# Moving a second conv pair of a hybrid decoder layer into the seven-product stage, with new orders at the start and around it

## The chip, the cores and the metric

The kernel runs on one core of a Trainium2 chip. The core has a matrix engine (TensorE, PE in the profile), a vector engine (VectorE, DVE), an activation engine (ScalarE, ACT), a general-purpose engine (GpSimd, POOL) and a queueing engine (SyncE, SP); 16 DMA engines carry transfers between its memory and the chip's. The metric is the time of one execution in microseconds on the device.

## The reference

One decoder layer of 1024 positions with a model width of 1024, all in float32 (cut to what matters):

```python
h = rms_norm(x, g_mix)
z = einsum("bsd,de->bse", h, w_in) + b_in          # 1024 -> 7168 columns
va, ga, xb, gb, sa, sb = split(z)                  # 1024, 1024, 1536, 1536, 1024, 1024
u = causal_depthwise_conv(va * sigmoid(ga), conv_a_w, conv_a_b)     # width 31
y_a = silu(layer_norm(u, ln_g, ln_b)) @ w_a_out
v = causal_depthwise_conv(xb, conv_b_w, conv_b_b)                   # width 4
v = rg_lru(v, ...)         # 16 heads of 96 channels, gates, h_t = a_t * h_(t-1) + b_t
y_b = (v * gelu(gb)) @ w_b_out
m = sigmoid(sa) * y_a + sigmoid(sb) * y_b
x = x + m @ w_o
f = square(relu(rms_norm(x, g_mlp) @ w_1))         # 1024 -> 4096
out = rms_norm(x + f @ w_2, g_final)
```

## The kernel before

**Matmuls.** Every matrix factor is split into a high and a low part, and a product is three matmuls: high by high, high by low, low by high. Weights are the stationary side (128x128), activations the moving side (128x512). Positions lie along the free axis.

**Tables.** `GA + j`, `VA + j`, `XB + t`, `GB + t`, `SA + j`, `SB + j` are numbers of column blocks of 128 of `z`. The in-projection has two parts. In the first, each block is one *slot* of plain matmuls (`chunk_mm`, L725, 48 of them into two banks). The table `CH` lists the blocks in order, `NC1` is their number, and slots `s` run from 3 on, as the first three blocks are made by `first_z` (L258) at the kernel's start. In the second part, blocks go in pairs listed in `ZPAIRS`, and each pair is made by a seven-product scheme (`z_mm`, L929): seven steps of 12 matmuls in place of two times 48. The scheme needs sums of weights (`zs`, on DVE), their split halves (`zo`), and sums of the activations (`xs`) split into `xs4` to `xs7`, in two halves each.

**Splitting.** `split_dma` copies the negated source into the low tile on ACT (L65), lets a POOL-issued DMA add the source to it (L66), and copies the high part on ACT (L67). For other tiles DVE subtracts the high part (L462 is a helper that issues queued vector work). So a `zo` tile is ready when the POOL-issued transfer has landed.

**Recurrent part.** Slots also hold the heads of the recurrent layer: gates on ACT (L542), and per group of three 128-channel tiles an exponential round (L558, L559), a root round (L566) and scans on DVE (`scan_tile`: L575, L576, L577, L578). `HS0` gives each head its slot, `EXP` the slots of the exponential rounds. A scanned tile goes to memory (`hd`) and comes back as `hb` to be multiplied with gelu of a `GB` block (L969, L972).

**Conv part.** `u_out` makes `u = (va + b) * sigmoid(ga + b)` (sigmoid on ACT at L587), and DVE does the width-31 convolution between other work (L637). The second part's `VA` pair does the same in `z_u` (L944).

**Order.** All of it is written out by hand and by a planner in the source: `clk` holds planned clocks of the engines, `later` queues vector work with a planned ready time and a planned cost, and `XS`, `ZX`, `ZL` are tables of steps at given slots. On the chip an engine executes its instructions in this order and waits on semaphores.

**Later stages.** After the second part come `yb` (L1129), `y_a` and the output projection (L1427), the up projection (`gu` products and `f` products, L1427 and L1709), and the down projection (L2002). `up_load` (L1664) loads a block of `w_1` as `raws[i, kk]`; `GX` is a table of its extra steps.

Of the kernel before, what the change touches and what calls it, by code (L numbers as in the profile page):

```python
# [30 lines left out]
def trunk_kernel(ctx: ExitStack, tc: tile.TileContext, x, xt_in, xt_eo, vecs, w_in, w_a_out, w_b_pl, w_b_sq,  # L31
# [97 lines left out]
    gmix = cp.tile([P, 16], F32, name="gmix")  # L129
    nc.sync.dma_start(gmix[:, 0:8], vecs[:, 0:8])  # L130
    nc.gpsimd.dma_start(vec, vecs)
# [31 lines left out]

    load_w0(0)
    for c2 in range(4):
        load_xc(0, c2)
# [18 lines left out]

    def x_square(t, eng):
# [5 lines left out]
        if eng is nc.vector:  # L192
            nc.vector.scalar_tensor_tensor(a, a, 1.0, a, ALU.mult, ALU.mult, accum_out=ss)
        else:
            nc.scalar.activation(a, a, AF.Square, accum_out=ss)
# [47 lines left out]
    def first_w(i, part):  # L243
        if part == "h":
            if i < 2:
                wh = wp.tile([P, 8, P], F32R, tag="wh", name=f"w{i}_h")
                wl = wp.tile([P, 8, P], F32R, tag="wl", name=f"w{i}_l")
            else:
                wh, wl = (T(f"w{i}_{n}", F32R).rearrange("p (k c) -> p k c", c=P) for n in "hl")
            w0.append((wh, wl))  # L250
            z0.append(PS(f"z{16 + i}"))
            nc.scalar.activation(wh, raw0[i], AF.Copy)
        else:
            nc.vector.tensor_tensor(w0[i][1], raw0[i], w0[i][0].bitcast(F32), ALU.subtract)

    def first_z(i, hf, k, which):
# [78 lines left out]
    with tc.manual_schedule(engines={mybir.EngineType.Activation, mybir.EngineType.DVE,  # L335
# [4 lines left out]

        spare = PS("spare", "ps2")

# [37 lines left out]
        for c in range(9):  # L380
# [5 lines left out]
            if 3 <= c < 7:  # L386
                x_square(c - 3, nc.scalar)
            if c:
# [195 lines left out]

    def u_gate(j, ps):
        ut[j] = u = T(f"u{j}")
        nc.scalar.activation(u.rearrange("p (o n) -> p o n", o=2), ps.rearrange("p (n o) -> p o n", o=2),  # L587
                             AF.Sigmoid, bias=bin_c[:, GA + j:GA + j + 1])
        return at("A", 1.11)

    def u_mul(j, ps, ready=0):
        uv = ut[j].rearrange("p (o n) -> p o n", o=2)
        later(ready, 1.28, nc.vector.scalar_tensor_tensor, uv, ps.rearrange("p (n o) -> p o n", o=2),
              bin_c[:, VA + j:VA + j + 1], uv, ALU.add, ALU.mult)
        fresh.append(j)

    def u_out(j, psv, psg):
        u_mul(j, psv, u_gate(j, psg))

# [191 lines left out]
    def z_get(n, f):  # L791
# [17 lines left out]
    with tc.manual_schedule(engines=ENGINES):  # L809
        for s in range(3, NC1):  # L810
# [33 lines left out]
            elif c >= GA:  # L844
                if CH[s] == c - GA + VA:
                    u_gate(c - GA, zps[s - 1])
                else:
                    u_out(c - GA, zps[s - 2], zps[s - 1])
            w_parts(s + 1)
# [170 lines left out]

    ZX = {0: ((x_parts, 1, 7),), 2: ((x_parts, 1, 5),), 4: ((x_parts, 1, 4),)}
    H_AT = {2: (0, 0), 5: (1, 1), 3: (0, 1), 4: (1, 0)}
    with tc.manual_schedule(engines=ENGINES):
# [155 lines left out]
        z_get(3, z_lhs)  # L1179
        u_mul(NU - 1, zps[NC1 - 1])  # L1180
        vector_work(clk["V"])
# [588 lines left out]
    def g_get(n, f):  # L1770
# [511 lines left out]
```

## Time and profile before

| What | Value |
|---|---|
| median of 3 runs | 1531.3 us (1531.1 to 1531.85) |
| profiled execution, own time | 1531.15 us |
| its span | 1529.4 us, clock 0.999 |
| PE busy | 1519.5 us, 6722 matmuls |
| DVE busy | 1200.0 us |
| ACT busy | 928.3 us |
| POOL busy | 192.3 us |

The span is the time between the first and the last instruction that the profile shows; the execution's own time is 1.75 us longer. By matmul lines, the stages lie so on the time axis: start and first three blocks to 43 us; plain slots 43 to 339; second part of the in-projection 339 to 627; `yb` 627 to 757; `y_a` and output projection 757 to 907; up 907 to 1217; down 1217 to 1522. *Z* below is the moment when the second part begins on PE, 339.29 us.

A row of the timeline has start, duration, engine, line, operation, output<-input, the tile's shape, a count where several equal ones are merged, and in brackets the engine's idle time before it with what ended it.

### The profile page before, as it was taken

Reading aid. Unit: us, or ns where it says so; the run is one execution under the profiler, and the core shown is the slowest. Engines: PE = TensorE matmul, PEld = TensorE weight load, DVE = VectorE, ACT = ScalarE, POOL = GpSimd, SP = SyncE. Lnnn points to the kernel's source line nnn. Section 1 sums busy time; section 2 is a strip of 40 time slices with the busy share of each in tenths; the row PEclk is TensorE's granted clock in tenths of the full one; section 3 lists DMA queues with packets and bytes.
Section 4 is the critical chain, followed back from the end, with each engine's and each line's share of the span. In section 5 each row is a group of like instructions: output and inputs, shape, how many; then the busy total and the mean of one; then the engine's idle time right before and its main releaser. Section 6 shows DMA issues by size and latency. Waiting matters only on the chain.

```text
span 1529.4 us, 18963 instructions
## 1 busy us (share of the span) xinstructions
PE 1519.5 (99%) x6722; PEld 1251.2 (82%) x6722; DVE 1200.0 (78%) x1636; ACT 928.3 (61%) x1299; POOL 192.3 (13%) x228
## 2 busy tenths in 40 slices
PE   9999999999999999999999999999999999999998
PEld 7878887888888888888888887888888888888886
DVE  6899996998999997788869879755555387777777
ACT  6748688576566667645575777554444455545475
POOL 0111011022222222000022332000000000101010
PEclk9999999999999999999999999999999999999999
DMA  9766779797997889964879897333333974776465
GB/s 352 188 146 154 184 159 204 196 258 209 265 261 173 186 207 271 297 226 119 269 201 302 188 205 195 138 122 111 111 111 111 302 265 131 177 211 169 107 123 153
DMA packets 130799, 296.53 MB, mean 194 GB/s; under 512 B 12896, under 2 KB 34912, under 8 KB 130704
## 3 DMA queue, kind: packets, MB, share of 16 engines
q1 hardware_dynamic: 98960, 215.92, 42.0%
q0 software_dynamic: 31600, 79.15, 28.1%
q8 instruction: 52, 0.85, 0.2%
q14 instruction: 43, 0.35, 0.1%
q10 hardware_dynamic: 144, 0.26, 0.0%
HBM read 149.79 MB, written 60.82 MB: 138 GB/s over the span
## 4 chain that ended last, share of the span: by engine, by line
PE 96%; issue 2%; DVE 1%; POOL 1%; DMA 0%; ACT 0%; POOLq 0%; ACTq 0%
PE z L725 16%; PE z L258 2%; PE d1b L2002 2%; PE d2b L2002 2%; PE d0b L2002 2%; PE d3b L2002 2%; PE d0e L2002 1%; PE d3e L2002 1%; PE d3a L2002 1%; PE d2e L2002 1%; PE d2a L2002 1%; PE d1e L2002 1%; PE d1a L2002 1%; PE d0a L2002 1%; PE rg L532 1%
## 5 line engine op out<-in xcount | busy, mean ns | idle before, releaser
L725 PE MATMUL z<-xh,win_h 128*128 128x512 f32 x368 | 115.4, 391 | 0.0
L725 PE MATMUL z<-xl,win_h 128*128 128x512 f32 x368 | 114.9, 390 | 0.0
L637 DVE SCALAR_TENSOR_TENSOR y<-u,vec,y 128x511 f32<-128x511 f32 (+14 forms) x120 | 88.2, 735 | 0.0
L725 PE MATMUL z<-xh,win_l 128*128 128x512 f32 x368 | 87.4, 389 | 0.0
L637 DVE SCALAR_TENSOR_TENSOR yt<-u,vec,yt 128x511 f32<-128x511 f32 (+6 forms) x112 | 82.5, 736 | 0.0
L637 DVE SCALAR_TENSOR_TENSOR y<-yt,csum,y 128x511 f32<-128x511 f32 (+6 forms) x112 | 82.4, 736 | 0.0
L725 PEld LDWEIGHTS z<-xh,win_h 128*128 128x128 f32 x368 | 69.1, 188 | 16.0 <-ACT win_h L67 0.5
L725 PEld LDWEIGHTS z<-xl,win_h 128*128 128x128 f32 x368 | 69.1, 188 | 14.9
L725 PEld LDWEIGHTS z<-xh,win_l 128*128 128x128 f32 x368 | 69.1, 188 | 14.6
L542 ACT ACTIVATE g<-rg,vec 96x1024 f32<-96x1024 f32 x32 | 35.5, 1110 | 72.9 <-PE rg L534 72.8
L1697 ACT ACTIVATE o<-s 128x512 fp32r<-128x512 f32 x56 | 33.7, 623 | 45.7 <-DVE s L1681 26.4
L66 POOL DMA_DIRECT2D zo<-zw x45 | 39.2, 871 | 133.8 <-ACT zo L65 110.4
L483 DVE SCALAR_TENSOR_TENSOR v<-xb,vec,v 128x1023 f32<-128x1023 f32 (+2 forms) x36 | 46.2, 1282 | 6.3 <-ACT v L474 5.3
L66 POOL DMA_DIRECT2D db_10l<-br x4 | 3.5, 877 | 339.6 <-DMA br<-in_w_dram 254.4
L66 POOL DMA_DIRECT2D win_l<-win_raw x23 | 20.0, 868 | 194.0 <-ACT win_l L65 155.9
L65 ACT ACTIVATE zo<-zw 128x512 fp32r<-128x512 f32 x45 | 28.2, 626 | 24.3 <-PE z10f L929 2.1
L1219 DVE TENSOR_TENSOR o<-s,o 128x512 fp32r<-128x512 f32 x56 | 37.2, 683 | 1.3 <-ACT o L1697 1.3
L66 POOL DMA_DIRECT2D zo<-zs x30 | 26.4, 879 | 75.9 <-ACT zo L65 63.8
L67 ACT ACTIVATE zo<-zw 128x512 fp32r<-128x512 f32 x45 | 27.9, 621 | 0.0
L578 DVE TENSOR_TENSOR_SCAN g<-a,g 128x1024 f32<-128x1024 f32 x12 | 27.5, 2291 | 0.4
L66 POOL DMA_DIRECT2D ga<-gsa x8 | 7.0, 874 | 161.0 <-DMA m<-mbd 150.8
L1219 DVE TENSOR_TENSOR o<-w_raw,o 128x512 fp32r<-128x512 f32 x38 | 25.9, 683 | 0.0
(3182 smaller groups left out, 4912.0 us busy)
## 6 DMA issues: line engine op xcount, KB each, us to landing
w_raw<-in_w_dram SPq DMA_DIRECT2D x34, 512.0 KB, 5.7
br<-in_w_dram SPq DMA_DIRECT2D x32, 512.0 KB, 6.1
ar<-fd SPq DMA_DIRECT2D x32, 512.0 KB, 7.0
zw<-in_w_in_dram SPq DMA_DIRECT2D x28, 512.0 KB, 6.9
win_raw<-in_w_in_dram SPq DMA_DIRECT2D x23, 512.0 KB, 5.0
win_l<-win_raw POOLq DMA_DIRECT2D x23, 512.0 KB, 5.2
zo<-zw POOLq DMA_DIRECT2D x45, 256.0 KB, 5.7
gates<-zg SPq DMA_DIRECT2D x32, 256.0 KB, 4.1
```

The source lines that it names most:

```text
L65: nc.scalar.activation(l, src, AF.Copy, scale=-1.0)
L66: nc.gpsimd.dma_start(l, src, accum_op=ALU.add)
L67: nc.scalar.activation(h, src, AF.Copy)
L258: nc.tensor.matmul(z0[i][:, HALVES[hf]], w0[i][w][:, k, :], xpart(a, hf, k), start=k == 0 and which == "hh", stop=k == 7 and which == ("hl ...
L483: nc.vector.scalar_tensor_tensor(v[:, d:S], a[:, 0:S - d], cbw_c[:, w * 12 + t:w * 12 + t + 1], v[:, d:S], ALU.mult, ALU.add)
L542: nc.scalar.activation(a, gps.pop((n, gi))[:HD, :], AF.Sigmoid, bias=(ba_c, bx_c)[gi][:, n:n + 1])
L578: nc.vector.tensor_tensor_scan(i, a, i, 0.0, ALU.mult, ALU.add)
L637: nc.vector.scalar_tensor_tensor(o[:, k:], a[:, 0:HS - k], c, o[:, k:], ALU.mult, add)
L725: nc.tensor.matmul(zps[s][:, HALVES[hf]], w[:, k, :], xw[k][part][hf], start=n == 0, stop=n == 23)
L1219: tt(l, src, h.bitcast(F32), ALU.subtract)
L1697: nc.scalar.activation(o[:, 0], src, AF.Copy)
L2002: nc.tensor.matmul(o, a, b, start=start and n == 0, stop=stop and n == len(todo) - 1, skip_group_check=not start or not stop)
```

## The change

1. The pair `GA + 6`, `VA + 6` leaves the plain slots (`NU` 7 to 6, `NC1` 26 to 24) and becomes a pair of the second part (15 pairs to 16). The second part's order mixes gate (`SA`), conv (`VA`) and recurrent (`GB`) pairs where before all `GB` pairs came first.
2. The plain slots are put in another order. The heads lose one of their two gaps, and the last exponential rounds start at slots 17 and 21 instead of 18 and 22.
3. Parts of the activation sums (`x_parts`) and the scan of tile 11 go from the slots into the second part.
4. At the start the first weight block and the first activation block are loaded in halves from two queues, the first split is made in halves, one of four squares goes from ACT to DVE, 14 small decay operations go behind the squares, and there are 9 idle matmuls for 13.
5. In the up stage, `raws[2, 0]` and `raws[3, 0]` are kept instead of loaded again, and the other halves of these blocks are loaded earlier (`up_load(2, (1,))`, `up_load(3, (1,))`).

```diff
-    load_w0(0)
-    for c2 in range(4):
+    nc.sync.dma_start(raw0[0][:, 0:4], w_in[16, :, 0:4])
+    nc.scalar.dma_start(xc[0][:, HALVES[0]], xt_in[0, 0, :, HALVES[0]])
+    nc.sync.dma_start(gmix[:, 0:8], vecs[:, 0:8])
+    nc.scalar.dma_start(raw0[0][:, 4:8], w_in[16, :, 4:8])
+    nc.sync.dma_start(xc[0][:, HALVES[1]], xt_in[0, 0, :, HALVES[1]])
+    for c2 in range(1, 4):
...
+    def first_half(n):
+        k = slice(4 * n, 4 * n + 4)
+        h, l = (a[:, k] for a in w0[0])
+        nc.scalar.activation(h, raw0[0][:, k], AF.Copy)
+        nc.vector.tensor_tensor(l, raw0[0][:, k], h.bitcast(F32), ALU.subtract)
...
-        idle_mm(13)
+        idle_mm(9)
         first_w(0, "h")
-        first_w(0, "l")
+        first_half(0)
         for c in range(8):
             x_plain(c)
             x_plain_low(c)
+            if c == 2:
+                first_half(1)
...
         first_w(2, "h")
         first_w(2, "l")
+        for t in range(4, 8):
+            x_square(t, t == 6)
         decay_on(14)
-        for t in range(4, 8):
-            x_square(t, nc.scalar)
...
-    CH = [XB, VA, GA, XB + 1, XB + 2, VA + 1, GA + 1, XB + 3, XB + 4, XB + 5, VA + 2, GA + 2]
-    CH += [XB + t for t in range(6, 12)] + [c for j in range(3, 7) for c in (VA + j, GA + j)]
-    NU = 7
-    CH[-2:] = CH[:-3:-1]
+    CH = [XB, VA, GA, XB + 1, XB + 2, VA + 1, GA + 1, XB + 3, XB + 4, XB + 5, XB + 6, XB + 7, XB + 8]
+    CH += [VA + 2, GA + 2, XB + 9, XB + 10, XB + 11] + [c for j in range(3, 6) for c in (VA + j, GA + j)]
+    NU = 6
...
-    ZPAIRS = [GB + 2 * i for i in range(6)] + [VA + 7] + [SA + 2 * i for i in range(4)]
+    ZPAIRS = [GB, GB + 2, SA, GB + 4, VA + 6, GB + 6, SA + 2, VA + 7, GB + 8, SA + 4, GB + 10, SA + 6]
     ZPAIRS += [SB + 2 * i for i in range(4)]
...
-    HS0 = [4 + n + (n > 3) + (n > 7) for n in range(NH)]
+    HS0 = [4 + n + (n > 3) for n in range(NH)]
-    XS = {NC1 - 5: ((x_load, 0),), NC1 - 4: ((x_sum, 0),), NC1 - 3: ((x_load, 1), (x_parts, 0, 6)),
-          NC1 - 2: ((x_sum, 1), (x_parts, 0, 7, 5)), NC1 - 1: ((x_parts, 0, 4), (x_parts, 1, 6))}
+    XS = {NC1 - 4: ((x_load, 0),), NC1 - 3: ((x_sum, 0),), NC1 - 2: ((x_load, 1), (x_parts, 0, 6)),
+          NC1 - 1: ((x_sum, 1), (x_parts, 0, 7))}
...
-    ZX = {0: ((x_parts, 1, 7),), 2: ((x_parts, 1, 5),), 4: ((x_parts, 1, 4),)}
+    ZX = {0: [(x_parts, 1, 6)], 1: [(x_parts, 1, 7)], 2: [(x_parts, 0, 5)], 3: [(x_parts, 1, 5)], 4: [(x_parts, 0, 4)], 5: [(x_parts, 1, 4)]}
+    ZX.setdefault(6, []).append((later, 0, 4.8, scan_tile, 11))
...
             src = raws[i, 0][:, 4 * (p - 1):4 * p, :]
-            if p == 2 and i > 1:
-                del raws[i, 0]
...
-        4: ((g_t, "u", 0, 2), (g_t, "u", 1, 2)), 5: ((g_parts, "u", 6, 0),),
+        4: ((up_load, 2, (1,)), (up_load, 3, (1,)), (g_t, "u", 0, 2), (g_t, "u", 1, 2)), 5: ((g_parts, "u", 6, 0),),
```

The order of instructions shows what the planner makes of it. Names there carry buffer numbers behind the last underscore, and the new kernel's lines are 5 to 14 higher than the old one's for the same statement.

**DVE at the start**, where the small decay operations (`sm`) begin; `w2_l` is the third weight block's low part, `x6` one of the four blocks whose squares give the first row scale. Before:

```order
L284 TENSOR_SCALAR sm_146<-sm_146 128x12
L254 TENSOR_TENSOR w2_l_243<-w2_raw_103,w2_h_242 128x1024
L286 SCALAR_TENSOR_TENSOR sm_146<-sm_146 128x12
L288 SCALAR_TENSOR_TENSOR sm_146<-sm_146 128x12
L290 MEMSET sm_146 128x12
```

And now:

```order
L296 TENSOR_SCALAR sm_148<-sm_148 128x12
L260 TENSOR_TENSOR w2_l_243<-w2_raw_105,w2_h_242 128x1024
L198 SCALAR_TENSOR_TENSOR x6_111,stx1_247<-x6_111 128x1024
L298 SCALAR_TENSOR_TENSOR sm_148<-sm_148 128x12
L300 SCALAR_TENSOR_TENSOR sm_148<-sm_148 128x12
L302 MEMSET sm_148 128x12
```

The square of `x6` stands on DVE ahead of the 14 decay operations, which in both kernels stand ahead of the row scale's first step (`stx1`).

**DVE at the border of the two parts**: `g0_11`, `g1_11` are the last scanned tile, `xs6l`, `xs7l` low parts of activation sums, `zs1` to `zs4` weight sums of pairs 0 and 1, `u5`, `u6` conv inputs. Before:

```order
L575 SCALAR_TENSOR_TENSOR g0_11_2366<-a11_2520,g0_11_2366 128x1024
L576 MEMSET g0_11_2366 128x1
L577 TENSOR_TENSOR g1_11_2411<-g0_11_2366,g1_11_2411 128x1024
L578 SCALAR_TENSOR_TENSOR g1_11_2411<-a11_2520,g1_11_2411 128x1024
L462 TENSOR_TENSOR xs6l_1_2769<-xs22_1_2597,xs6h_1_2768 128x1024
L462 TENSOR_TENSOR zs1_0_2797<-zw0_0_2606,zw0_1_2608 128x512
L462 TENSOR_TENSOR zs2_0_2798<-zs1_0_2797,zw0_0_2606 128x512
L462 TENSOR_TENSOR zs3_0_2799<-zw0_0_2606 128x512
L462 SCALAR_TENSOR_TENSOR u6_2753<-z25_2704,vec_87,u6_2753 128x1024
L462 TENSOR_TENSOR xs7l_1_2834<-xs12_1_2596,xs7h_1_2833 128x1024
L462 TENSOR_TENSOR zs3_1_2855<-zw1_0_2610 128x512
```

And now:

```order
L589 SCALAR_TENSOR_TENSOR g0_10_2191<-a10_2438,g0_10_2191 128x1024
L476 TENSOR_TENSOR zs1_0_2644<-zw0_0_2444,zw0_1_2446 128x512
L590 MEMSET g0_10_2191 128x1
L476 TENSOR_TENSOR zs2_0_2645<-zs1_0_2644,zw0_0_2444 128x512
L591 TENSOR_TENSOR g1_10_2241<-g0_10_2191,g1_10_2241 128x1024
L476 TENSOR_TENSOR zs3_0_2646<-zw0_0_2444 128x512
L592 SCALAR_TENSOR_TENSOR g1_10_2241<-a10_2438,g1_10_2241 128x1024
L476 TENSOR_TENSOR xs7l_0_2612<-xs12_0_2333,xs7h_0_2611 128x1024
L476 SCALAR_TENSOR_TENSOR u5_2658<-z22_2468,vec_87,u5_2658 128x1024
L476 TENSOR_TENSOR xs6l_1_2683<-xs22_1_2529,xs6h_1_2682 128x1024
L476 TENSOR_TENSOR zs3_1_2704<-zw1_0_2448 128x512
```

The scan ahead of the first weight sums is tile 10 where it was tile 11, `zs1_0` to `zs3_0` stand inside it, and `xs7l_0`, `u5` and `xs6l_1` stand between it and `zs3_1`.

**SP in the up stage**, around the last transfers of the residual rows (`x1d`). Before:

```order
L1585 DMA x1d_5412<-x1r6_7845 128x1024
L1585 DMA x1d_5412<-x1r7_7863 128x1024
L1486 DMA fd_5413<-f11_0_7992 128x512
L1486 DMA fd_5413<-f11_1_8012 128x512
L1486 DMA fd_5413<-f11_2_8040 128x512
L1486 DMA fd_5413<-f11_3_8066 128x512
L1664 DMA w1_4_raw_8199<-in_w_1_dram 128x1024
L1664 DMA w1_5_raw_8201<-in_w_1_dram 128x1024
L1664 DMA w1_6_raw_8295<-in_w_1_dram 128x1024
```

And now:

```order
L1594 DMA x1d_5438<-x1r6_7871 128x1024
L1594 DMA x1d_5438<-x1r7_7889 128x1024
L1673 DMA w1_5_raw_8014<-in_w_1_dram 128x1024
L1673 DMA w1_7_raw_8016<-in_w_1_dram 128x1024
L1495 DMA fd_5439<-f11_0_8022 128x512
```

The second loads of `w1_4` and `w1_6` are gone, and `w1_5` and `w1_7` are issued before the four `fd` transfers instead of behind them.

More of the change, by code (lines that the diff above doesn't have):

```diff
@@ L129, in trunk_kernel @@
     gmix = cp.tile([P, 16], F32, name="gmix")
-    nc.sync.dma_start(gmix[:, 0:8], vecs[:, 0:8])
     nc.gpsimd.dma_start(vec, vecs)
@@ L162, in load_w0 @@
             nc.sync.dma_start(raw0[i], w_in[(16, 0, 8)[i]])
-    load_w0(0)
-    for c2 in range(4):
+    raw0.append(wp.tile([P, 8, P], F32, tag="raw", name="w0_raw"))
+    xc.append(T("xc00"))
+    nc.sync.dma_start(raw0[0][:, 0:4], w_in[16, :, 0:4])
[4 more added lines that the diff above has]
+    for c2 in range(1, 4):
         load_xc(0, c2)
@@ L184, in trunk_kernel, with x_square @@
     rs_x = {}
-    def x_square(t, eng):
+    def x_square(t, dve=False):
         hf, i = divmod(t, 4)
@@ L191, in x_square @@
         a, ss = xt[(t + 4) % 8], rs_x[hf][:, 0, i:i + 1]
-        if eng is nc.vector:
+        if dve:
             nc.vector.scalar_tensor_tensor(a, a, 1.0, a, ALU.mult, ALU.mult, accum_out=ss)
@@ L339, in trunk_kernel @@
         nc.scalar.activation(warm[:, 0:1], warm[:, 1:2], AF.Sqrt)
-        spare = PS("spare", "ps2")
+        spare = PS("spare")
         def idle_mm(n):
@@ L386, in trunk_kernel @@
             if 3 <= c < 7:
-                x_square(c - 3, nc.scalar)
+                x_square(c - 3)
             if c:
@@ L583, in trunk_kernel, with u_out @@
     ysum = []
[L585 to L594, printed above, removed]
+    def u_out(j, psv, psg):
+        u = T(f"u{j}")
+        uv = u.rearrange("p (o n) -> p o n", o=2)
+        nc.scalar.activation(uv, psg.rearrange("p (n o) -> p o n", o=2), AF.Sigmoid,
+                             bias=bin_c[:, GA + j:GA + j + 1])
+        later(at("A", 1.11), 1.28, nc.vector.scalar_tensor_tensor, uv,
+              psv.rearrange("p (n o) -> p o n", o=2), bin_c[:, VA + j:VA + j + 1], uv,
+              ALU.add, ALU.mult)
+        ut[j] = u
         fresh.append(j)
-    def u_out(j, psv, psg):
-        u_mul(j, psv, u_gate(j, psg))
     NE = WA // 2 + 1
@@ L844, in trunk_kernel @@
             elif c >= GA:
[L845 to L848, printed above, removed]
+                u_out(c - GA, zps[s - 2], zps[s - 1])
             w_parts(s + 1)
@@ L1179, in trunk_kernel @@
         z_get(3, z_lhs)
-        u_mul(NU - 1, zps[NC1 - 1])
+        u_out(NU - 1, zps[NC1 - 2], zps[NC1 - 1])
         vector_work(clk["V"])
```

3 lines of the change are left out of this document (2 added, 1 removed).

## The prediction

> **What bounds the kernel now.** I read the page first (busy times), then PE's waits, then the chain of waits, then timelines of the four places where the change moves something: the start, the second exponential round, the border of the in-projection's two parts, and the up stage. The page's busy times, with the share of the span and the instructions:
>
> ```profile
> PE 1519.5 (99%) x6722; PEld 1251.2 (82%) x6722; DVE 1200.0 (78%) x1636; ACT 928.3 (61%) x1299; POOL 192.3 (13%) x228
> ```
>
> PE's waits on others, for the whole span, and the head of the chain of waits:
>
> ```profile
> PE spare L345 <- POOL ones L113: 1.6, 1, 1.6
> PE f0d L1709 <- DMA o<-s: 0.8, 1, 0.8
> ```
>
> ```profile
> PE 96%; issue 2%; DVE 1%; POOL 1%; DMA 0%; ACT 0%; POOLq 0%; ACTq 0%
> ```
>
> PE is busy 99% of the span, and its only waits of any size are 1.6 us at the very start and 0.8 us in the up stage. So the time falls with the number of matmuls, and every other edit can cost (a new wait of PE) or save at most the two waits shown. The question is how close to a wait PE runs at the places that the change touches.
>
> **Matmuls.** From the chain: a step of the seven-product scheme, and a run of plain matmuls.
>
> ```profile
> 301.16 38.12 PE z L725 x168
> 372.83 2.72 PE z2a L929 x12
> ```
>
> That is 38.12/168 = 0.227 us for a plain matmul and 2.72/12 = 0.227 for one of a step. The change takes 2 x 48 = 96 plain matmuls away and adds a pair of 7 x 12 = 84. 12 x 0.227 = 2.7 us less, on the engine that sets the end: **-2.7**. The four idle matmuls that go stand before the first load has landed and are worth nothing by themselves.
>
> **The start.** The rows that carry it are the first product on PE, the third square on ACT, the first and the last of 14 decay operations and the first step of the row scale on DVE and the matmul that spreads it:
>
> ```profile
> 7.17 0.70 PE L258 MATMUL z<-xh,w_h 128*128 128x512 f32 x1
> 8.12 3.88 ACT L227 ACTIVATE xh<-xc,gmix 128x512 fp32r<-128x512 f32 x6 [0.44 <-DMA xc<-in_xt_dram]
> 15.17 1.22 DVE L254 TENSOR_TENSOR w_l<-w_raw,w_h 128x1024 fp32r<-128x1024 f32 x1
> 16.31 0.17 DVE L286 SCALAR_TENSOR_TENSOR sm<-sm 128x12 f32<-128x12 f32 x1
> 17.09 1.06 ACT L195 ACTIVATE x<-x 128x1024 f32<-128x1024 f32 x1 [0.15 <-DMA x<-in_x_dram]
> 18.80 0.17 DVE L293 TENSOR_TENSOR sm<-sm 128x12 f32<-128x12 f32 x1
> 19.54 0.17 DVE L202 TENSOR_SCALAR stx<-stx 128x4 f32<-128x4 f32 x1 [0.58 <-ACT x L195]
> 20.98 0.39 PE L258 MATMUL z<-xl,w_h 128*128 128x512 f32 x1
> 21.50 1.13 PE L217 MATMUL rb<-rd,ones 128*128 128x128 f32 x8
> ```
>
> Halves bring the first product forward, by an estimated 1.2 us (half of the first weight block is half a transfer). But the activations come one after the other: ACT waits for them from 8.12 us on. The bytes ahead of the fourth block are the same in both kernels, so the first block row is still finished at about the same time, and the gain is used up before the row scale. There the order on DVE counts. Before, the 14 decay operations ran from 16.31 to 18.97 us beside ACT's squares and the scale began at 19.54. Now the square of `x6` comes first; it can begin when `x6` has landed (17.09 at the latest; I take 16.6, as the first transfers are issued earlier) and takes about what a row of that shape takes, 1.22. Then come the 14 operations at their measured 2.66. 16.6 + 1.2 + 2.66 = 20.5, so the scale begins 0.9 us later, and with it `rb` (21.50), where PE waits already: its last matmul before was issued at 20.98. Nothing covers it: **+0.9**. Bounds: -0.5 (everything lands earlier by what four idle matmuls and the halves save) and +1.2 (`x6` not before 17.09).
>
> **The second exponential round** now starts a slot earlier, so that the evacuation of an `XB` block falls into the slot behind it. Rows of before, the gates, the head's matmul that needs them, and one such evacuation:
>
> ```profile
> 242.32 1.10 ACT L471 ACTIVATE xb<-z,vec 128x1024 f32<-128x1024 f32 x1
> 243.45 1.25 ACT L474 ACTIVATE v<-xb,vec 128x1024 f32<-128x1024 f32 x1
> 262.07 1.09 ACT L542 ACTIVATE g<-rg,vec 96x1024 f32<-96x1024 f32 x1
> 265.29 0.40 PE L532 MATMUL rg<-vth,rgh 96*96 96x512 f32 x1
> ```
>
> The gate ends at 263.16, 2.1 us ahead of the matmul that takes over its bank. 1.10 + 1.25 = 2.35 us more on ACT in that slot leaves 0.2 uncovered: **+0.2**, bounds 0 (ACT's waits for PE elsewhere in the slot take it up) and 0.8.
>
> **The border.** Between the last exponential round and the second part lies one slot fewer. Rows of before:
>
> ```profile
> 310.33 1.04 ACT L65 ACTIVATE win_l<-win_raw 128x1024 fp32r<-128x1024 f32 x1
> 313.63 2.96 ACT L566 ACTIVATE g<-g 128x1024 f32<-128x1024 f32 x3
> 320.69 5.00 DVE L462 TENSOR_TENSOR xs<-xs,xs 128x1024 f32<-128x1024 f32 x4
> 335.40 2.29 DVE L578 TENSOR_TENSOR_SCAN g<-a,g 128x1024 f32<-128x1024 f32 x1
> 343.44 0.69 DVE L462 TENSOR_TENSOR zs<-zw 128x512 f32<-128x512 f32 x1
> 345.71 0.62 ACT L770 ACTIVATE zo<-zs 128x512 fp32r<-128x512 f32 x1
> 347.31 1.28 ACT L969 ACT_TABLE_LOAD   x1
> 348.60 0.69 ACT L969 ACTIVATE ze<-z0a,vec 128x512 f32<-128x512 f32 x1
> 352.16 0.89 POOL L66 DMA_DIRECT2D zo<-zs  x1 [10.20 <-ACT zo L65]
> 353.61 0.58 ACT L998 ACTIVATE z0e<-z0b 128x512 f32<-128x512 f32 x1 [0.27 <-PE z0e L918]
> 358.85 0.39 PE L929 MATMUL z0e<-xs5h,zo 128*128 128x512 f32 x1
> 362.02 0.62 PE L929 MATMUL z1b<-xs6h,zo 128*128 128x512 f32 x2
> ```
>
> The transfer that POOL issued at 352.16, as the DMA view gives it (KB, microseconds to landing), and one of the same size at 936.40 in the up stage:
>
> ```profile
> zo<-zs POOLq DMA_DIRECT2D x1, 256.0 KB, 6.8
> ```
>
> ```profile
> o<-s POOLq DMA_DIRECT2D x1, 256.0 KB, 3.8
> ```
>
> The three roots of the last group began at 313.63, Z - 25.7. The last exponential ended at 310.33, Z - 29.0; with a slot of 48 x 0.227 = 10.9 us fewer that is Z - 18.1. Behind it on ACT now stand a table load (1.28), a conv gate (about 1.1), two copies (1.04 each) and another load ahead of the roots: they begin near Z - 12.4, or a microsecond later if the copies wait for their load. Then DVE has tile 9 (4.8: 1.2 + 1.2 + 2.3 and a memset), `xs6l` (1.2), the sums (5.0), tile 10 (4.8), three weight sums (0.69 each), `xs7l`, `u5`, `xs6l` (1.2 each) before `zs3_1`: some 21 us after the first root, near Z + 10 where it stood at Z + 4.2 (343.44). ACT's copy for it (345.71 before) waits, and behind it in ACT's order stand two copies of `xs5`, a table load, the gelu, `zo1_6`'s copies and the copy `z0e<-z0b`. `zo1_6` is then issued near Z + 17.5 (before 352.16, Z + 12.9) and with 6.8 us lands at Z + 24.3; its third matmul stands at 362.02, Z + 22.7. The copy `z0e<-z0b` goes from 353.61 to near Z + 21, while PE asks for it at 358.85, Z + 19.6. That is 1.6 us for `zo1_6`, with the 1.4 for `z0e` contained in it, and an estimated 1.0 for the next transfer (`zo0_3`), whose copies stand behind on ACT, with the sums' `xs4` between: **+2.6**. Bounds: 0, if transfers land as the faster one of the two rows, and 5.0 with the later start of the roots (1.2) and as much again from the next transfer behind `zo1_6`. Tile 11's scan, moved behind, has the whole step of the later pairs as cover.
>
> **Table loads.** With gelu and sigmoid pairs mixed there are 24 loads more, 22 of them in the second part. Each is 1.28 us (347.31), the next instruction follows at once (348.60). The second part by busy time:
>
> ```profile
> 339.00:627.00 288.00, 288.00 (x1272) 238.51 (x1271) 256.40 (x386) 189.32 (x317) 66.66 (x77) 1.00 0.89 231
> ```
>
> ACT is idle 288 - 189 = 99 us of it, 4.5 us for each new load of 1.28: covered on the whole, with a cost only where a load stands just ahead of a bank that PE wants: **+0.2**, bounds 0 and 1.3 (one load uncovered). The Trainium skill, page "ScalarE: Activation LUTs", section "What ACT_TABLE_LOAD costs", speaks against the mixing: a switch costs the load and about 1.38 us of drain besides, 2.66 in all, so one should finish all work of one set first. The trace does not show the drain; by that figure 22 x 2.66 = 59 us would still fit into the idle time, and the sum would be the same 0.2 with an upper bound of 2.7.
>
> **The up stage.** Rows: the weight block `gu1_2`, PE's use of it, the one wait, the landing of `gu1_2`, the landing of the block that PE waits for (issued at 937.92, just before the loads of `w1_4` and `w1_5`), and the stretch in which the new loads come:
>
> ```profile
> 917.24 0.95 POOL L66 DMA_DIRECT2D gu<-w_raw  x1 [5.90 <-ACT gu L65]
> 925.32 0.72 PE L1427 MATMUL gu1a<-gu2h,gu 128*128 128x512 f32 x2
> 945.45 0.73 PE L1709 MATMUL f0d<-gu7h,o 128*128 128x512 f32 x2 [0.77 <-DMA o<-s]
> ```
>
> ```profile
> gu<-w_raw POOLq DMA_DIRECT2D x1, 256.0 KB, 8.0
> ```
>
> ```profile
> o<-s POOLq DMA_DIRECT2D x1, 256.0 KB, 7.5
> ```
>
> ```profile
> 920.00:924.00 4.00, 4.00 (x19) 3.30 (x18) 4.00 (x7) 3.15 (x7) 2.48 (x3) 1.00 1.07 280
> ```
>
> The wait at 945.45 goes, since the two loads beside it are moved away: -0.9 with the pace that is regained. But the loads of `w1_5` and `w1_7` (2 x 512 KB) now start near 917.3, beside `gu1_2`, which lands at 917.24 + 8.0 = 925.28, just when PE takes it (925.32), with the DMA engines full (share 1.07). 1 MB at 280 GB/s is 3.7 us; if the loads go ahead of it, PE waits 3.7, if they only share with what is left of it, 0.9. I take 2.0. **Sum +1.1**, bounds -0.9 and +2.8. The Trainium skill, page "DMA: Bandwidth & Descriptors", section "Queues, rings and completion order", has the DMA engines take packets from the queues in turn; by it the loads would push `gu1_2` by about its own remaining share, an estimated 1.4. No row here shows the two side by side.
>
> The convolution on DVE gets its last `u` later, but is needed only in `y_a`, behind 757 us; nothing is put down for it.
>
> **The sum** is -2.7 + 0.9 + 0.2 + 2.6 + 0.2 + 1.1 = +2.3, made against the profiled execution's 1531.15 (0.15 below the median of the runs): 1533.4. A measurement of this kernel can tell about 0.2% from no change, 3.1 us.
>
> **Rivals.**
> *Clean*: PE meets no new wait, as the planner's queued times leave it none. -2.7 for matmuls, -0.9 for the up stage, 0 to -0.5 at the start: 1527.3. For it: only two waits of PE in the whole span before, and the transfer of 256 KB that took 3.8. Against it: `gu1_2` comes with no slack at all, and DVE is 89% busy in the second part (256.40 of 288).
> *Border in full*: the roots begin at Z - 11.3 and the transfers keep their 6.8 us, one behind the other; PE pays 5.0 there in place of 2.6: 1535.8, slower. It decides from about 3.7 us at that border on, where the sum passes 1534.4. For it: everything on DVE there stands in one chain behind the roots.
> *Table loads on the path*: a third of the 22 loads stand ahead of a bank that PE wants, and PE pays 7 x 1.28 = 9: 1542. By the page's 2.66 it would be 7 x 2.66 = 19. Against it: 99 us of idle ACT.
>
> **How the numbers follow.** Chances: the sum as worked out 0.42, clean 0.27, border in full 0.26, table loads 0.05. The sum's own case spreads from 1529 to 1536 (its start and up terms by their bounds): 0.33 within 0.2% and 0.09 above. Clean is faster with 0.25 and just within with 0.02. The others are slower. So faster 0.25, same 0.35, slower 0.40. The range from 1526.5 to 1537.5 takes in the clean case with its start gain and the border in full with two microseconds of the up stage's bound; what it leaves out is the table loads and the ends, under 2 in 10.
>
> **What would show it.** Right: 12 matmuls fewer of the kept kind; `rb` near 22.4; a wait of PE between Z + 19 and Z + 26 on `z0e`, `zo1_6` or `zo0_3`; a wait at the third matmul that uses `gu1_2`; no wait at `f0d`. Wrong: no wait of PE longer than 0.3 us at any of these (then clean), waits behind table loads all over the second part, or waits at places that I have not named, such as the steps of a `VA` pair between two `GB` pairs.

## The result, and the profile after

The changed kernel takes 1543.98 us (median of 5 runs, 1542.96 to 1546.55) against 1531.25 us (1531.1 to 1531.85): a ratio of 1.0085, 95% interval 1.0073 to 1.0096. It is slower by 12.7 us, outside the range given. The profiled execution took 1544.11 us, its span is 1542.3 us. The head of its page and PE's waits (what PE waited for, in total, times, longest):

```profile
PE 1521.8 (99%) x6702; PEld 1248.2 (81%) x6702; DVE 1205.3 (78%) x1648; ACT 961.5 (62%) x1335; POOL 194.6 (13%) x231
```

```profile
PE z4a L939 <- DMA zo<-zw: 3.0, 1, 3.0
PE spare L357 <- POOL ones L113: 1.6, 1, 1.6
PE z15e L939 <- ACT zc L1016: 1.5, 1, 1.5
PE z0e L939 <- ACT z0e L1008: 1.3, 1, 1.3
PE z0f L939 <- DVE zc L476: 1.3, 1, 1.3
PE gu1a L1436 <- DMA gu<-w_raw: 1.0, 1, 1.0
PE z L270 <- ACT xh L232: 0.9, 2, 0.7
PE z0e L939 <- DMA zo<-zs: 0.7, 1, 0.7
PE gu3a L1436 <- DMA gu<-w_raw: 0.7, 1, 0.7
PE rb L222 <- DVE rd L213: 0.7, 1, 0.7
PE z0a L939 <- ACT z0b L1005: 0.4, 1, 0.4
```

Where one wait stood before besides that of the idle matmuls (`spare`), ten of 0.4 us or more stand now. PE has 20 instructions fewer (12 products, 8 rows of the 4 idle ones) and yet is busy 2.3 us longer, because matmuls at half rate count as busy for longer. They stand behind the largest wait, at the second step of pair 4 (`z4a`). Its PE rows, and then the busy row of the 20 us around it:

```profile
406.63 0.39 PE L939 MATMUL z4a<-xl,zo 128*128 128x512 f32 x1
410.03 1.22 PE L939 MATMUL z4a<-xh,zo 128*128 128x512 f32 x2 [3.00 <-DMA zo<-zw]
...
414.46 0.63 PE L939 MATMUL z3e<-xh,zo 128*128 128x512 f32 x1
414.88 0.63 PE L939 MATMUL z3e<-xl,zo 128*128 128x512 f32 x1
```

```profile
400.00:420.00 20.00, 17.00 (x63) 13.51 (x63) 14.84 (x24) 12.21 (x19) 3.06 (x4) 0.83 0.83 203
```

Behind the wait of 3.0 us the matmuls start 0.43 us apart (414.46 to 414.88) instead of 0.227, and the granted clock of this stretch is 0.83 (third number from the end). Thirteen of them at some 0.20 us extra are about 2.7 us.

Time that PE lost, from start to start of its matmuls over the pace of 0.227, by place (after less before):

| Place | Predicted | Traces |
|---|---|---|
| matmuls that are gone | -2.7 | -2.7 (by count: 96 plain less 84, at an unchanged pace) |
| start, up to `rb` | +0.9 | +1.1 (21.50 to 22.61) |
| slot of the second exponential round | +0.2 | +0.2 |
| border of the two parts | +2.6 | +4.7 (four waits) |
| pair 4, second step (`z4a`) | 0 | +5.9 (3.2 of wait, 2.7 of half rate) |
| last pair and first `yb` step (`z15e`, `yb0b`) | 0 | +2.1 |
| table loads | +0.2 | none seen |
| up stage | +1.1 | +1.0 |

Together 12.3 of the 12.9 us between the spans.

### The profile page after: what moved, and what is told of

Read it like the earlier page. It is cut to its first block, busy times and chain, and to the rows that moved or that the text cites. A ratio compares the mean times of both kernels' runs of the same rounds, so it can differ in the third digit from the quotient of the medians.

```text
span 1542.3 us, 19003 instructions
## 1 busy us (share of the span) xinstructions
PE 1521.8 (99%) x6702; PEld 1248.2 (81%) x6702; DVE 1205.3 (78%) x1648; ACT 961.5 (62%) x1335; POOL 194.6 (13%) x231
## 4 chain that ended last, share of the span: by engine, by line
PE 88%; DMA 4%; ACT 3%; DVE 2%; issue 2%; POOL 0%; SPq 0%; DVEq 0%; POOLq 0%; ACTq 0%
PE z L738 12%; PE d2b L2011 2%; PE d1b L2011 2%; PE d0b L2011 2%; PE d3b L2011 2%; PE d0e L2011 1%; PE d0a L2011 1%; PE d3e L2011 1%; PE d3a L2011 1%; PE d2e L2011 1%; PE d2a L2011 1%; PE d1e L2011 1%; PE d1a L2011 1%; PE z L270 1%; DMA xs<-xu 1%
## 5 line engine op out<-in xcount | busy, mean ns | idle before, releaser
L738 PE MATMUL z<-xh,win_h 128*128 128x512 f32 x336 | 105.5, 391 | 0.0
L738 PE MATMUL z<-xl,win_h 128*128 128x512 f32 x336 | 105.0, 390 | 0.0
L738 PE MATMUL z<-xh,win_l 128*128 128x512 f32 x336 | 79.9, 389 | 0.0
L738 PEld LDWEIGHTS z<-xh,win_h 128*128 128x128 f32 x336 | 63.1, 188 | 14.7 <-ACT win_h L67 0.4
L738 PEld LDWEIGHTS z<-xl,win_h 128*128 128x128 f32 x336 | 63.1, 188 | 13.7
L738 PEld LDWEIGHTS z<-xh,win_l 128*128 128x128 f32 x336 | 63.1, 188 | 13.4
L65 ACT ACTIVATE zo<-zw 128x512 fp32r<-128x512 f32 x48 | 30.1, 626 | 17.6 <-issue 7.5
L67 ACT ACTIVATE zo<-zw 128x512 fp32r<-128x512 f32 x48 | 29.8, 621 | 0.0
```

Of the source, the lines that this page charges most:

```text
L65: nc.scalar.activation(l, src, AF.Copy, scale=-1.0)
L67: nc.scalar.activation(h, src, AF.Copy)
L738: nc.tensor.matmul(zps[s][:, HALVES[hf]], w[:, k, :], xw[k][part][hf], start=n == 0, stop=n == 23)
```

## The experiments

All compare with runs of the kernel before on the same chip. The diffs are against the changed kernel, but for the two that start from the kernel before.

**The conv blocks' sums left out.** At the end of a conv block, SP writes its result (`yd`) and POOL adds it to a running sum (`ysum`).

```diff
         else:
-            nc.gpsimd.dma_start(ysum[0], acc, accum_op=add)
+            pass
```

> The changed kernel without the POOL-issued transfers that add each conv block's result to the running sum (ysum), so that sum holds the first block alone; all else as in the changed kernel. Theory A (conv ends): PE loses 5.9 us at the second step of pair 4 because its weight transfer (zo) is queued on POOL behind the ysum transfer of a conv block that has just ended; then that wait and the half-rate matmuls behind it go, the wait at the last pair (1.9 us) shrinks, and the time is about 1537. Theory B (table loads): the zo transfer is issued late because ACT's copies stand behind three table loads; then ysum matters little, the wait stays above 2 us, and the time is about 1543.

1535.4 us, ratio 1.0025 (1.0016 to 1.0035): 8.6 us less than the changed kernel. PE's longest waits behind that of the idle matmuls are these, with neither `z4a` nor `z15e` in the whole list:

```profile
PE z L270 <- ACT xh L232: 1.3, 2, 1.0
PE z0e L939 <- ACT z0e L1008: 1.3, 1, 1.3
PE z0f L939 <- DVE zc L476: 1.2, 1, 1.2
```

This is how POOL's queue stood around block 3's sum in the kernel before:

```profile
378.15 1.23 POOL L650 DMA_DIRECT2D ysum<-y  x1
382.15 0.87 POOL L66 DMA_DIRECT2D zo<-zw  x1 [2.77 <-DMA zo<-zw]
```

And in the changed kernel, at pair 4, with what the weight transfer behind the sum took:

```profile
397.00 0.87 POOL L66 DMA_DIRECT2D zo<-zs  x1 [2.17 <-ACT zo L65]
397.54 1.23 POOL L664 DMA_DIRECT2D ysum<-y  x1
398.53 1.16 POOL L66 DMA_DIRECT2D zo<-zw  x1
```

```profile
zo<-zw POOLq DMA_DIRECT2D x1, 256.0 KB, 11.5
```

The block's sum now stands 1.0 us ahead of the weight transfer that PE wants, where the next one followed 4.0 us later before. That transfer takes 11.5 us; with the sum left out, issued at 398.41, it took 7.4.

**The same sums, only later.** Nothing is left out.

```diff
+            if j in hold_sum:                       # {3: 2, 7: 99}
+                held_sum.append([hold_sum[j], acc])
+            else:
                 nc.gpsimd.dma_start(ysum[0], acc, accum_op=add)
...
             z_get(n + 4, z_lhs)
+            sums_out(n == len(zseq) + 1)
```

> The changed kernel with two of the eight running-sum transfers issued later on POOL: that of conv block 3 behind zo4_2 and zo3_3 instead of just ahead of zo4_2, that of block 7 behind the second part. Nothing is left out. Theory A1 (place in POOL's queue): the 5.9 us at pair 4 and the 1.9 us at pair 15 go, time about 1536, as without those transfers. Theory A2 (their bytes, wherever they are issued): zo5_1 or zo4_4, now behind it, is late instead, and PE still waits 1 us or more near pair 5; time 1538 to 1542.

1538.21 us, ratio 1.0045 (1.0030 to 1.0060). Both waits are gone. The weight transfer, issued at 398.40, now stands ahead of the sum (402.50) and lands in time:

```profile
zo<-zw POOLq DMA_DIRECT2D x1, 256.0 KB, 7.1
```

So what costs PE its time at pair 4 is that the sum is issued just ahead of the weight transfer (A1), and not that its bytes are moved at all. The profiled spans differ by 6.8 us: 5.9 are gained at pair 4 and 1.7 at the last pair, and 1.0 is lost at the first `yb` step (`yb0b`), where PE now loses 1.3. That last loss does not come from the new place of block 7's sum: the run below that leaves the sums alone and undoes start and up stage loses 1.2 there too. In both, ACT's copy that PE waits for stands right behind the split of `hg7`, which waits for its load.

**Sigmoid pairs behind the gelu pairs.**

```diff
-    ZPAIRS = [GB, GB + 2, SA, GB + 4, VA + 6, GB + 6, SA + 2, VA + 7, GB + 8, SA + 4, GB + 10, SA + 6]
+    ZPAIRS = [GB, GB + 2, GB + 4, GB + 6, VA + 6, GB + 8, GB + 10, VA + 7, SA, SA + 2, SA + 4, SA + 6]
```

> The changed kernel with its sigmoid (SA) pairs behind all gelu (GB) pairs: GB, GB+2, GB+4, GB+6, VA+6, GB+8, GB+10, VA+7, then SA and SB. Table loads of the second part fall from 24 to about 10. Theory B (table loads): no wait at pair 4, time about 1538. Theory A (conv ends): a conv block still ends in that stretch, so a wait of 1 to 3 us stays at pair 4 or a neighbour, time 1540 to 1544. The border's 4.7 us stay in both, except what the table load ahead of the first gelu has in it.

1541.05 us, ratio 1.0067 (1.0052 to 1.0082). No wait at pair 4, as theory B has it; but the order of the steps moved too: block 3's sum was issued at 402.65, behind the transfer of 398.78. So this run does not tell table loads from the collision. The run before does: there all table loads stand as in the changed kernel, and the wait is gone; from Z + 40 to Z + 290 PE loses nothing at all. Table loads are not the cause. The total fell by only 2.9 us, because the loss at the last pair grew from 1.7 to 4.0 us, half-rate matmuls included.

**The scans of tiles 10 and 11 later.**

```diff
-                    if 3 * g <= t < 3 * g + 3:
+                    if 3 * g <= t < min(3 * g + 3, 10):
-    ZX.setdefault(6, []).append((later, 0, 4.8, scan_tile, 11))
+    ZX.setdefault(4, []).append((later, 0, 4.8, scan_tile, 10))
+    ZX.setdefault(8, []).append((later, 0, 4.8, scan_tile, 11))
```

> The changed kernel with the scan of tile 10 also moved into the second part (step 4) and that of tile 11 from step 6 to step 8. If the border's 4.7 us come from DVE's chain behind the roots (tiles 9 and 10 ahead of the weight sums), 4.8 us less in that chain leave about 1 us of it: time about 1540. If the border waits come from ACT's own order (table load, gelu, copies) or from the transfers' 7 us, it stays at 4 or more: about 1543.5.

1550.23 us, ratio 1.0129 (1.0113 to 1.0146): worse, which neither case had. The wait for the copy `z0e` is gone, as DVE's chain is 4.8 us shorter there; in its place PE waits 3.6 us for `zc`, since the scan of tile 11 now stands right ahead of it on DVE, begun late behind a wait for a transfer:

```profile
348.02 0.69 DVE L476 TENSOR_TENSOR zs<-zw 128x512 f32<-128x512 f32 x1 [3.07 <-DMA zo<-zs]
...
351.27 2.29 DVE L592 TENSOR_TENSOR_SCAN g<-a,g 128x1024 f32<-128x1024 f32 x1
353.48 0.66 DVE L476 TENSOR_TENSOR zc<-zc,z0f 128x512 f32<-128x512 f32 x1
```

The border loses 8.4 us in all here in place of 4.7, and the last pair 3.9 in place of 1.7.

**Tile 11 alone at step 12, and the two `w1` loads three steps later.**

```diff
-    ZX.setdefault(6, []).append((later, 0, 4.8, scan_tile, 11))
+    ZX.setdefault(12, []).append((later, 0, 4.8, scan_tile, 11))
...
-        4: ((up_load, 2, (1,)), (up_load, 3, (1,)), (g_t, "u", 0, 2), ...
+        4: ((g_t, "u", 0, 2), ...
-        7: ((g_parts, "u", 5, 1), ...
+        7: ((up_load, 2, (1,)), (up_load, 3, (1,)), (g_parts, "u", 5, 1), ...
```

> The changed kernel with the scan of tile 11 queued at step 12 of the second part instead of step 6, and the early loads of w1_5 and w1_7 at step 7 of the up stage instead of step 4. If the fourth border wait (1.4 us, z0f behind DVE's zc) is caused by the scan that stands ahead of zc on DVE, it goes and the other border waits (0.5, 1.5, 0.9) stay; if DVE's earlier backlog causes it, it stays above 0.8. If the loads' place beside gu1_2 caused the up stage's 2.2 us, these go, and the old 1 us at f0d does not come back, since only one load of w1_4's kind is left beside it. Time about 1540.5; with both wrong 1544.

1548.3 us, ratio 1.0115 (1.0099 to 1.0132). The fourth border wait is gone, so the scan ahead of `zc` caused it; but the third one grew from 0.7 to 3.6 us, and the last pair lost 4.1 in place of 1.7. For the third, SP shows what moved. In the changed kernel, and then in this run:

```profile
350.04 0.32 SPq L593 DMA_DIRECT2D hd<-g  x1
350.45 0.38 SPq L1000 DMA_DIRECT2D hb<-hd  x1
350.93 0.74 SPq L756 DMA_DIRECT2D zw<-in_w_in_dram  x1
```

```profile
338.90 1.28 SPq L1000 DMA_DIRECT2D hb<-hd  x2
340.28 0.70 SPq L756 DMA_DIRECT2D zw<-in_w_in_dram  x1
```

The scan's write (`hd<-g`) held SP's queue until 350; with it out of the way the next loads start 10 us earlier and share the DMA engines with `zo0_3`, which took 8.7 us in place of 5.9. That the sharing made it longer is read from these rows; no run tests it alone. In the up stage both `gu` waits went, and 1.6 us of new losses came at `f0c` and `f1c`.

**Start and up stage undone.**

```diff
-        for t in range(4, 8):
-            x_square(t, t == 6)
         decay_on(14)
+        for t in range(4, 8):
+            x_square(t)
...
             src = raws[i, 0][:, 4 * (p - 1):4 * p, :]
+            if p == 2 and i > 1:
+                del raws[i, 0]
...
-        4: ((up_load, 2, (1,)), (up_load, 3, (1,)), (g_t, "u", 0, 2), ...
+        4: ((g_t, "u", 0, 2), ...
```

> The changed kernel with two edits undone: the decay operations go ahead of the squares again and all squares to ACT; and in the up stage the early loads of w1_5 and w1_7 are left away and w1_4, w1_6 loaded again. If the order on DVE made the row scale late, rb comes back from 22.6 to about 21.6 us (-0.8 to -1.0). If the early loads made gu1_2 and gu3_2 late, 2.2 us of waits there go and the 1.05 us at f0d come back (-1.2). Together about 1542. If either was innocent, its waits stay where they are.

1541.02 us, ratio 1.0063 (1.0048 to 1.0078). `rb` starts at 21.61, without a wait, against 22.61:

```profile
21.38 0.39 PE L270 MATMUL z<-xl,w_h 128*128 128x512 f32 x1
21.61 0.60 PE L222 MATMUL rb<-rd,ones 128*128 128x128 f32 x4
```

What stood on DVE was the cause: the square with the 14 operations behind it, which this run undoes together. The loads by halves, still in this run, are worth nothing at `rb` (21.50 before). The two `gu` waits are gone and 0.5 us are left at `f0d`.

**The named edits together, mixed and unmixed.** Sums later, tile 11 at step 12, `w1` loads at step 7, old order of the squares; then the same with the sigmoid pairs behind the gelu pairs and only block 7's sum moved.

> The changed kernel with four edits together: running sums of blocks 3 and 7 later, scan of tile 11 at step 12, w1_5 and w1_7 loaded at step 7, decay operations ahead of the squares and all squares on ACT. By the ledger 1544.0 - 7.8 - 1.4 - 2.2 - 0.9 = 1531.7, the border's remaining 3 us of waits standing against the 2.7 us of matmuls saved. If the terms are not additive (DVE's work only moves), 1534 or more.

> As the run before, with the sigmoid pairs behind the gelu pairs and only block 7's sum moved. Table loads fall by about 14. If table loads matter only through pair 4's late copy, it is the same as the run before, about 1531.7; if they cost a little everywhere, it is 1 us or more faster; if gelu pairs in a row fill the DMA engines, it is slower by waits on zo.

1542.8 us, ratio 1.0072 (1.0057 to 1.0087), and 1541.29 us, ratio 1.0067 (1.0052 to 1.0082). Tile 11 at step 12 brings its 3.9 us wait here too, and half-rate matmuls behind it, so both miss the 1531.7. The first also loses 1.9 us at `yb0b` and 1.2 at `z7a`, the second 1.9 at `yb0b`. The intervals overlap: no difference of the mixing can be told.

**The changed kernel mended where that worked.** Block 3's sum two transfers later, start and up stage undone, tile 11 left at step 6. Block 7's sum is written five steps into the `yb` stage in the source, but the trace shows that it did not move.

> The changed kernel with the places undone that the ledger names: running sum of conv block 3 issued two transfers later, that of block 7 five steps into the yb stage, decay operations ahead of the squares and squares on ACT, up stage as before. The scan of tile 11 stays at step 6. By the ledger 1544.0 - 5.9 - 1.9 - 1.0 - 1.5 = 1533.7, still slower than before, because the border's 4.4 us are more than the 2.7 us of matmuls saved. If the border's waits are the only net loss left, it lands at 1533 to 1534.5; if block 7's sum costs elsewhere (1.3 us at the first yb step in an earlier run), 1535.

1536.35 us (1534.37 to 1538.27), ratio 1.0031 (1.0021 to 1.0042); the profiled execution took 1534.86. What is left are the border's waits and 1.4 us at `yb0b`:

```profile
PE z0f L950 <- DVE zc L476: 1.3, 1, 1.3
PE z0e L950 <- ACT z0e L1019: 1.3, 1, 1.3
PE yb0b L1151 <- ACT yb0a L1171: 1.2, 1, 1.2
PE z0e L950 <- DMA zo<-zs: 0.7, 1, 0.7
```

Block 7's sum stands between the same two weight transfers on POOL as in the changed kernel (there 612.78, 613.80 and 617.65):

```profile
605.55 0.87 POOL L66 DMA_DIRECT2D zo<-zw  x1 [1.70 <-ACT zo L65]
606.66 0.87 POOL L604 DMA_DIRECT2D ysum<-y  x1 [0.25 <-DVE y L666]
610.41 0.89 POOL L66 DMA_DIRECT2D zo<-zs  x1 [2.88 <-ACT zo L65]
```

And yet the last pair loses only 0.2 us here. Over all kernels made from the changed one, itself included, the last pair loses nothing in the four whose sum of block 7 is left out or stands behind the second part, and 0.2 to 4.7 us in the ten where it stays. So the sum has a part in that loss, but what sets its size is open.

**Two parts of the change alone, on the kernel before.**

```diff
-            if p == 2 and i > 1:
-                del raws[i, 0]
```

> The kernel before with one part of the change alone: raws[2, 0] and raws[3, 0] are kept, so the second loads of w1_4 and w1_6 go; w1_5 and w1_7 are loaded where they were. If the wait at f0d (1.05 us) came from both loads beside it, about half of it goes (0.5 us were left in the run that undid the other parts): 1530.7. If it came from the blocks' own transfer, no change: 1531.2.

1529.86 us (1529.44 to 1530.43), ratio 0.9990 (0.9981 to 0.9999): 1.7 us less by the medians, and the best kernel of the study, though its interval only just leaves out no change. In the profiled executions the up stage is 0.8 us shorter. The wait at `f0d` is gone, but that alone says little, as it is gone in the next run too, which still loads these blocks twice and loses 1.2 us in that stage, at `gu1a` and `f1d`. The end of PE's waits:

```profile
PE z L258 <- ACT xh L227: 0.3, 1, 0.3
PE gu1a L1425 <- DMA gu<-w_raw: 0.2, 1, 0.2
```

```diff
-    CH = [..., XB + 3, XB + 4, XB + 5, VA + 2, GA + 2]
-    CH += [XB + t for t in range(6, 12)] + ...
+    CH = [..., XB + 3, XB + 4, XB + 5, XB + 6, XB + 7, XB + 8]
+    CH += [VA + 2, GA + 2, XB + 9, XB + 10, XB + 11] + ...
```

> The kernel before with another part alone: the new order of the plain blocks (six XB in a row, then VA+2, GA+2), heads and exponential rounds in their old slots, 26 blocks. Theory: the new order only moves DVE's idle time from 240-280 us to 180-220 us, and the conv ends come later than before by 20 us at most; what makes them late in the changed kernel is the 20 us of slots that are gone. Then no new waits, 1531 within 1 us. Rival: the order itself starves the convolution and shifts its ends into the zo transfers; then PE waits 1 us or more in the second part, 1533 or more.

1531.62 us, ratio 1.0001 (0.9992 to 1.0010). The order of the blocks alone costs nothing and leaves block 3's sum in its place (378.67 against 378.15), though it moves those of blocks 1 and 2 back by 9 and 17 us. In the changed kernel block 3's sum is issued at Z + 79 us, before at Z + 39. What moved it is thus the rest of the new first part: the two slots that are gone, the heads' new slots or the moved sums. No run takes these apart.

**The border, taken apart.** First the scan of tile 9 left out:

```diff
+        if t != 9:
             nc.vector.scalar_tensor_tensor(r, a, 1.0, r, ALU.add, ALU.mult)
...
             nc.vector.tensor_tensor_scan(i, a, i, 0.0, ALU.mult, ALU.add)
```

> The changed kernel without the four DVE instructions of the scan of tile 9 (4.8 us), which stand first in DVE's chain at the border; tile 9 then holds its unscanned input. All other instructions keep their order. Theory (DVE's chain behind the roots delays zs3_1, ACT's copy for it, and all that stands behind on ACT): the waits at the border on z0b (0.5), on the copy z0e (1.4) and on zo0_3 (0.9) all go or fall below 0.3 each; the fourth (z0f behind the scan of tile 11, 1.4) falls too if that scan starts earlier. Border together below 1.5 instead of 4.7. Rival (transfers of 6 to 7 us, or ACT's own order with the table load in it): the waits stay above 3 together.

1544.14 us, ratio 1.0079 (1.0063 to 1.0096): no gain, so the theory as stated fell. The border loses 5.6 us here. DVE had 4.8 us less to do and spent them waiting, mostly for the second half of the activation blocks:

```profile
314.90 1.23 DVE L476 TENSOR_TENSOR xs<-xs,xs 128x1024 f32<-128x1024 f32 x1 [2.48 <-DMA xs<-xu]
317.83 2.48 DVE L476 TENSOR_TENSOR xs<-xs,xs 128x1024 f32<-128x1024 f32 x2 [1.71 <-DMA xs<-xu]
```

Those loads take 10 to 15 us in the changed kernel (the third of them, issued at 301.24):

```profile
xs<-xu SPq DMA_DIRECT2D x1, 512.0 KB, 15.2
```

So the loads were moved a slot earlier, alone, then with tile 9 left out, then in the mended kernel:

```diff
-    XS = {NC1 - 4: ((x_load, 0),), NC1 - 3: ((x_sum, 0),), NC1 - 2: ((x_load, 1), (x_parts, 0, 6)),
+    XS = {NC1 - 4: ((x_load, 0),), NC1 - 3: ((x_sum, 0), (x_load, 1)), NC1 - 2: ((x_parts, 0, 6),),
```

> The changed kernel with the second four xs loads issued a slot earlier, ahead of the zw loads. If the loads alone hold the border, the x sums no longer wait and all border waits fall to below 2 us together (1541). If loads and DVE's chain are about equally long, the chain takes over: border 3.5 to 4.5 (1543). The zw loads come later, so zo0_1 and zo0_2 may be late: then a new wait in the second part's first steps.

> Both: the second xs loads a slot earlier and the scan of tile 9 left out of DVE (tile 9 holds its unscanned input). If chain and loads are the two limits of the border, both are gone, zs3_1 comes some 5 us earlier, and the waits on z0b, the copy z0e and zo0_3 fall below 1 us together. If ACT's own order or the transfers of 6 to 7 us hold it, they stay above 2.5 together.

> The changed kernel with all named places mended (running sums of blocks 3 and 7 later, decay operations ahead of the squares, up stage as before) and the second xs loads a slot earlier. If the border falls below 2 us, 1536.4 - 2.5 = 1534 or less; to come under the kernel before it would need no border waits at all and none at the first yb step. I expect 1535.

The second of these, with both limits gone: 1539.52 us, ratio 1.0057 (1.0039 to 1.0075). The waits for the copy `z0e` and for `zo0_3` are gone; 0.5 us at `z0a` and 0.8 at `z0f` stay, and the border loses 1.9 us in place of 4.7. Another 2.8 us of the gain are not owed to the edit: the wait at pair 4 had no half-rate matmuls behind it in this run. `zs3_1` started at Z + 8 (328.10, Z at 319.97) where it had stood at Z + 11 (330.10, Z at 318.85). So the border is held by two limits of about equal length, DVE's chain and the loads; in the changed kernel DVE waits only 0.76 us for the loads within its chain, so earlier loads alone could free little. That case was not measured cleanly, although the border still lost 4.4 and 4.1 us in the two runs with the loads moved and the scan kept. The loads alone, 1555.53 us, ratio 1.0161 (1.0143 to 1.0179), and in the mended kernel, 1546.55 us, ratio 1.0102 (1.0086 to 1.0118), were much worse: SP's queue now issues the write of tile 8 (`hd<-g`, at 301.83) behind 4 MB of loads, ACT waits for it, and PE for ACT:

```profile
312.95 1.28 ACT L603 ACT_TABLE_LOAD   x1 [12.04 <-DMA hd<-g]
```

```profile
PE z L738 <- ACT win_h L67: 9.3, 1, 9.3
```

The late write is not enough as a cause. In the run without tile 9's scan it is issued at 302.38, behind the same loads, and in the changed kernel it lands at 307.7; in neither does ACT wait for it at that instruction, which runs at 302.17 and 301.04. New in these two runs is the wait itself. A tile that takes over the memory from which the write still reads would explain it; no run shows that.

No order was found that does all the work and frees the border without a new wait.

## Why the prediction was wrong

- **Matmuls** (-2.7): right.
- **Start** (+0.9): right, and for the reason given: the third square ran on DVE from 17.03, the 14 operations behind it, and the scale's first step stood at 20.76 (predicted 20.5). The halves brought the first product forward by 1.2 us (7.17 to 5.99), and nothing was left of that at `rb`, as forecast.
- **Second exponential round** (+0.2): right, 0.2 at 255.75, where a gate on ACT ends at 255.70.
- **Border** (+2.6): mechanism right, size too small. With Z at 318.85, `zs3_1` stood at Z + 11.2 (predicted Z + 10), the copy `z0e` at Z + 21.4 (Z + 21), and PE lost 1.4 there and 0.9 at `zo0_3` (at Z + 29, later than the Z + 26 that was named), near what was worked out; `zo1_6` had no wait of its own. The step that failed is "Tile 11's scan, moved behind, has the whole step of the later pairs as cover": it stands on DVE two short operations ahead of `zc`, which PE wants, and costs 1.4; another 0.5 came at `z0a`, and about 0.1 behind each wait. Nor were the roots the only head of the chain: the loads of the activation blocks were as late. DVE and ACT there in the changed kernel:

```profile
316.59 3.74 DVE L476 TENSOR_TENSOR xs<-xs,xs 128x1024 f32<-128x1024 f32 x3 [0.76 <-DMA xs<-xu]
330.10 0.69 DVE L476 TENSOR_TENSOR zs<-zw 128x512 f32<-128x512 f32 x1
330.82 0.63 ACT L783 ACTIVATE zo<-zs 128x512 fp32r<-128x512 f32 x1 [3.42 <-DVE zs L476]
340.23 0.58 ACT L1008 ACTIVATE z0e<-z0b 128x512 f32<-128x512 f32 x1
```

- **Convolution** (0): this is the step that did most to put the time out of the range, 6.5 us above its end. "The convolution on DVE gets its last `u` later, but is needed only in `y_a`" looked at who needs the results and not at what a block issues at its end: two transfers of 512 KB, one of them on the queue that carries the weights. That cost 5.9 us at pair 4, shown by the sums left out and by the sums later. The prediction had named the steps of a `VA` pair between two `GB` pairs as a sign of being wrong, and pair 4 is that pair (`VA + 6`), but its sum had no term for it. At the last pair 1.7 us more were lost, with block 7's sum in it but its size open, as said above. DVE waits there for `yd` and ACT for a gate's write:

```profile
625.16 1.23 DVE L476 TENSOR_TENSOR hb7l<-hb,hb7h 128x1024 fp32r<-128x1024 f32 x1 [5.04 <-DMA yd<-y]
628.15 0.77 ACT L990 ACTIVATE zg<-zu,vec 128x512 f32<-128x512 f32 x1 [2.63 <-DMA gates<-zg]
```

- **Table loads** (+0.2): no cost that the runs could tell, as the idle time of ACT suggested. With all of them in place and the sums later, PE lost nothing from Z + 40 to Z + 290.
- **Up stage** (+1.1): mechanism right, the size partly by luck. 2.0 us were put down for `gu1_2` alone; PE lost 1.1 there and 1.0 at `gu3`, which was not named, against the 1.1 at `f0d` that went. Of the two edits there, keeping the blocks is the useful one and the early loads the harmful one.
- **A wait counted once**: no term had the half rate behind a long wait, 2.7 us here. That is partly chance: behind waits of 2.7 and 2.8 us at the same place in two other kernels there was none.

## What to carry to other kernels

A moved piece of vector work moves the transfers that it ends with: for every block whose end shifts, find which queue its last DMA stands on and what follows it there. Shortening a stage by 22 of 296 us came with the slack of several other things gone (roots, activation loads, the convolution's transfers), and mends uncovered new waits; a saving of 2.7 us on PE needs all its neighbours' slack counted before it is one. A change made of many parts is worth taking apart: a piece of one of its five parts, alone, was the fastest kernel measured, though its interval only just leaves out no change. And an edit should be looked up in the trace before its result is read: one moved sum had not moved.

## What the runs showed of the hardware

- Behind long waits PE may run at half rate, but not always. Over all profiles of this study, from 40 us on, 16 gaps of 2.5 us or more lie from the start of one matmul to the next. Behind 13 of them, 5 to 12 matmuls stand 0.43 us apart, in some only from the third to sixth matmul on; behind three (3.11, 3.20 and 2.60 us) there are none. Of three gaps of 2.1 to 2.4 us, the one of 2.40 (a wait of 2.0 us, at pair 3 in the run with both scans later) has them too; the granted clock over the 10 us around it is 0.83, which is 3.4 us at half.
- The Trainium skill, page "TensorE: Matmul & The Clock Gate", Part 1, has the clock halved after an idle window of about 3.4 us that runs freely. That a gap of 2.60 us brought half rate in one kernel and not in another agrees with a window that runs freely; that a wait of 2.0 us can be enough is shorter than the figure.
- A POOL-issued transfer of 256 KB took 11.5 us behind one of 512 KB that adds to its target, and 7.1 us ahead of it, issued at nearly the same moment of the program (398.53 and 398.40).
